# Attention by pairs of heads and one token tile, heads alternating between halves of the TensorE array

## The chip, the cores and the metric

The kernel runs on one core of one Trainium2 chip. The metric is the device time of one execution in microseconds, as the median of several executions; lower is better. TensorE (PE in the profile) multiplies, VectorE (DVE) and ScalarE (ACT) do the elementwise work and empty PSUM, GpSimd (POOL) does little here, and SyncE (SP) issues the DMAs.

## The reference

Two blocks follow each other on 256 tokens of width 1024. The first has a layer with a recurrence and a retention, and a layer with sparse attention (NSA); each has an FFN. The second has two layers with two attention branches of four heads each (`a` and `d`), a Fourier branch and a spatial gate; its first layer does the same for 256 context tokens, whose keys and values both layers attend to. Cut to what the change touches:

```python
# retention, a chunk of 128 tokens at a time, 8 heads of 64
s = jnp.einsum('bhid,bhjd->bhij', qf, kf) * inner_decay
o = jnp.einsum('bhij,bhjd->bhid', s, vf) + ...
# NSA: 16 heads of 64, 4 groups of keys; selected blocks, window, compressed keys
p_slc = jax.nn.softmax(s, axis=-1)...
o_slc = jnp.einsum('bgrqkl,bgqkld->bqgrd', p_slc, vg)
p_win = jax.nn.softmax(jnp.where(band, s, NEG), axis=-1)
o_win = jnp.einsum('bgrqk,bkgd->bqgrd', p_win, vw)
o = gb[..., 0:1] * o_cmp + gb[..., 1:2] * o_slc + gb[..., 2:3] * o_win
# second block, per branch; k and v are context and own tokens; sink in branch d
s = jnp.einsum('bqkgd,bnkd->bkgqn', q, k)
p = jax.nn.softmax(jnp.concatenate([s, s_sink], axis=-1), axis=-1)[..., :-1]
o = jnp.einsum('bkgqn,bnkd->bqkgd', p, v)
```

## The kernel before, in words

All weights are streamed from HBM in pieces of 512 KB, and each piece is split into two float32r parts, `whi` by ACT and `wlo` by DVE (lines 339 and 340). A product in these parts is three matmuls (`mm3`, lines 420 to 422: low times high, high times low, high times high). A product in plain float32 (`mm`, line 425) is one matmul in the code; the trace has two MATMUL rows for it. Most of the time goes to such products on the whole 128 by 128 array.

A head has 64 columns. Scores contract over 64 features, so their matmuls use half of the array's rows: the first half for the even head of a pair, the second for the odd one (`r0`). The product with the values has 64 output features, so it uses half of the array's columns. The trace writes a whole-array matmul `128*128`, one on half of the rows `64*128`, one on half of the columns `128*64`.

- **Retention** (`hybrid`, lines 759 to 773): a loop over 8 heads; scores into a bank of PSUM `P` (line 764), times the decay on DVE (766 and 767), times the values (769 to 771). Two heads go with each of four steps of the product for `g`.
- **NSA** (`nsa`, from 994): a unit is one head, the even or the odd one (`half`) of a pair `p`, and both token tiles: `scores(p, half)` makes them, 256 keys wide for the first and 512 wide for the second, in two `P` banks. `softmax(p, half, s)` takes the maximum with the mask (1012), the exponential (1015), and scales by the gates (1021), in the buffer `C3` (`Es`). Then come six transposes (1038) into two `Q` banks, copies to SBUF by ACT (1041) and DVE (1042), and the product with the values into `po`, the free half of a score bank. After the second unit of a pair, `split` writes `po` to `oT`. The scores of unit k + 2 and the softmax of unit k + 1 are issued around the work of unit k.
- **Attention of the second block** (`attend`, from 1136): the same with units `(p, half)` and both token tiles in a unit; `X` is the main stream, `C` the context's. In `X` the scores are 512 wide over two key tensors, 12 matmuls of 256 columns for each unit in two `R` banks; the values' products (`weigh`) are four of 256 columns. In `C` both token tiles of a head share one bank.

What runs beside it: generators yield after each piece of work, and `beside`, `bg` and `side_by` step the context's stream and the modulation beside the main path. The tile framework's scheduler then sets the order of each engine's instructions; each engine takes them in that order and waits on semaphores.

Of the kernel before, what the change touches and what calls it, by code (L numbers as in the profile page):

```python
# [13 lines left out]
OP = mybir.AluOpType  # L14
# [10 lines left out]
# ---------------------------------------------------------------- host side: layout and constants  # L25
# [197 lines left out]
def _bd(w):  # L223
    """[2n, 64, 64] -> [128, n * 128], pairs on a block diagonal."""
# [8 lines left out]
def _params(i):  # L233
    """Per-partition parameters and small operands, each [128, n]."""
# [29 lines left out]
def _rows(i):  # L264
    """Vectors along the free axis, to be spread over the partitions by DMA."""
# [30 lines left out]
# ---------------------------------------------------------------- device side  # L296

class Weights:
    """A stream of weights: DMA of each piece, and its split into two float32r parts."""
# [7 lines left out]
    def keep(self, name, tags):  # L307
        """The next pieces of this name go to buffers of their own."""
# [37 lines left out]
def kernel(ctx: ExitStack, tc: tile.TileContext, x_in, ctx_in, wmain, wctx, wada, params, rows, tabs, out,  # L346
# [14 lines left out]
    # -- buffers  # L361
# [10 lines left out]
    class Env:  # L372
        """What a stream of work uses for itself: weights, a ring of short rows, and banks of PSUM."""
# [13 lines left out]
    def group(keys, src, place, tag, pool_=None):  # L387
        """neighbouring tables in one DMA; a view of each"""
# [18 lines left out]
    # -- small helpers  # L407
# [6 lines left out]
    def after_marks():  # L414
        """what follows is issued after the last split"""
# [31 lines left out]
    def beside(g, *others):  # L447
        """the work g, with a step of the others after each of its own"""
# [12 lines left out]
    def behind(seen):  # L461
        """what follows is issued after the first split of a weight since"""
# [8 lines left out]
    def rms_factor(env, src, junk, after=None):  # L471
        """One token tile [128, 1024]: the factor of each row."""
# [53 lines left out]
    def f_out(env, o, xf, name):  # L526
        """128 output features on partitions: o [128, 256]."""
# [6 lines left out]
    def f_two(env, xf, name, acc=None):  # L534
        """256 output features, two blocks side by side in one bank."""
# [30 lines left out]
    class Out:  # L566
        """1024 output features along the free axis; the rows of the weight come one tile at a time."""
# [19 lines left out]
        def flush(self, gs):  # L587
            """the products held, for these groups: token tile g % 2 of operand g // 2"""
# [24 lines left out]
    def rope(dst, src, tc_, ts_, h, b, c, ta_, tb_):  # L613
        """dst = src * cos + swapped(src) * sin; rows of h heads, each b blocks of two halves of c."""
# [12 lines left out]
    # ------------------------------------------------------------ first block  # L627
# [26 lines left out]
    def recur_params(ga_b, gx_b, lam):  # L654
        # softplus(-lam) = max(-lam, 0) + log1p(exp(-|lam|)), log1p by the series of atanh
# [21 lines left out]
    def hybrid(hook):  # L677
# [23 lines left out]
        # recurrent branch  # L701
# [13 lines left out]
        def recur():  # L715
# [13 lines left out]
            # a = exp(-X), tp = tanh(X/2): 1 - a = tp (1 + a), which keeps its digits where X is small  # L729
# [15 lines left out]
        # retention branch  # L745
# [13 lines left out]
        def retention():  # L759
            for h in range(8):  # L760
                r0 = slice(64 * (h % 2), 64 * (h % 2) + 64)
                s = psum("P")
                mm(s[:, 0:256], kT[r0, h // 2, 0:128], qT[r0, h // 2, :])
                mm(s[:, 256:384], kT[r0, h // 2, 128:256], qT[r0, h // 2, 128:256])
                st = X.tmp(384)
                dve.tensor_mul(st[:, :256], s[:, :256], decay[:, h * 256:(h + 1) * 256])
                dve.tensor_mul(st[:, 256:], s[:, 256:384], decay[:, h * 256:h * 256 + 128])
                hc = slice(64 * h, 64 * h + 64)
                mm(ro[0][:, hc], st[:, 0:128], vv[:, 0, hc])
                mm(ro[1][:, hc], st[:, 128:256], vv[:, 0, hc], True, False)  # L770
                mm(ro[1][:, hc], st[:, 256:384], vv[:, 1, hc], False, True)
                yield

        ret = retention()
        o = yield from beside(t_out(X, xf, "g", 512), ret, ret, rec)
# [27 lines left out]
        gn = group_norm(rp)  # L803
# [19 lines left out]
    def nsa(hook, pre):  # L823
# [8 lines left out]
        def rope16(v, t, h):  # L832
            """in place on the first 16 of 64 columns of h heads; v [128, h * 64]"""
# [6 lines left out]
        # keys: columns of kT are slc1 slc0 win0 win1; the compressed ones of two groups on a block diagonal  # L840
# [14 lines left out]
        # compressed keys and values  # L855
# [67 lines left out]
        # queries  # L923
# [23 lines left out]
        def compressed():  # L947
            """the probabilities over the compressed keys, all heads at once, times the gates"""
# [45 lines left out]
        def scores(p, half):  # L994
            """of token tiles 0 and 1; the first leaves half a bank"""
            r0 = slice(64 * half, 64 * half + 64)
# [7 lines left out]
        def softmax(p, half, s):  # L1004
            """the probabilities of both token tiles times the gates"""
            E = Es[:, half]
            mx, rs = X.small(4, "mx"), X.small(4, "rs")
            parts = [(2 * t + i, s[t][:, i * w:i * w + w], E[:, c + i * w:c + i * w + w], m)
                     for t, w, c, ms in ((0, 128, 0, (nsa_m[:, 128:256],) * 2), (1, 256, S, (nsa_m[:, 128:384], nsa_m[:, 0:256])))
                     for i, m in enumerate(ms)]  # L1010
            for k, z, e, m in parts:
# [574 lines left out]
```

## Time and profile before

| | |
|---|---|
| executions, us | 1486.92, 1484.84, 1478.87 |
| median, us | 1484.84 |
| span of the profiled execution, us | 1487.6 |
| PE busy in the span | 1434.1 us, 96% |
| PEld (weight loads) busy | 1274.3 us, 86% |
| DVE busy | 969.4 us, 65% |
| ACT busy | 715.2 us, 48% |
| mean granted TensorE clock | 0.985 |

The span runs from the first to the last instruction of one execution; a time for what lies around it is not shown, and the median of the three executions lies 2.8 us below it. A PE row's duration is how long one matmul takes from start to end. Matmuls are pipelined, so what one costs in a row of them is the distance from its start to the next one's start.

### The profile page before, as it was taken

How to read it: one execution, taken by the hardware profiler on the slowest of the kernel's cores; microseconds unless marked ns; L12 is line 12 of the kernel's file. 1: busy time of each engine (PE TensorE's matmuls, PEld its weight loads, DVE VectorE, ACT ScalarE, POOL GpSimd, SP SyncE). 2: the span in 40 equal slices, each digit the busy share in tenths (PEclk: the TensorE clock that was granted, in tenths of full speed). 3: DMA queues.
4: the chain of work that ended last, by engine and by line, in shares of the span. 5: the costliest groups of instructions: out<-in, count | busy, mean ns of one | idle time of the engine just before them, and what ended most of it. 6: DMA issues, size and time to landing. Idle time of an engine off the chain costs nothing. (4 is left out here: it accounts for less than half of the span.)

```text
span 1487.6 us, 23997 instructions
## 1 busy us (share of the span) xinstructions
PE 1434.1 (96%) x9591; PEld 1274.3 (86%) x9591; DVE 969.4 (65%) x1747; ACT 715.2 (48%) x1206; POOL 39.2 (3%) x46
## 2 busy tenths in 40 slices
PE   7998999999999999999998999999999999999998
PEld 6777889988797668999887888899999878879997
DVE  7867887645676767768786765443443667764566
ACT  5643435556455654544445565333333346653443
POOL 0000000000100000000000100000000001100000
PEclk9999999999998999999999999999999999999999
DMA  8635776545453007676775442133333526413563
GB/s 288 205 120 188 249 239 231 171 139 175 131 149 108 1 30 225 216 240 229 233 254 177 150 128 86 59 120 107 113 103 126 156 62 185 146 55 101 184 186 126
DMA packets 65745, 230.30 MB, mean 155 GB/s; under 512 B 7776, under 2 KB 9312, under 8 KB 65376
## 3 DMA queue, kind: packets, MB, share of 16 engines
q1 hardware_dynamic: 65632, 228.76, 48.2%
q8 instruction: 75, 1.23, 0.3%
q14 instruction: 38, 0.31, 0.1%
HBM read 227.68 MB, written 1.05 MB: 154 GB/s over the span
## 5 line engine op out<-in xcount | busy, mean ns | idle before, releaser
L340 DVE TENSOR_TENSOR wlo<-raw,whi 128x1024 fp32r<-128x1024 f32 (+2 forms) x325 | 392.3, 1210 | 181.0 <-ACT whi L339 179.3
L339 ACT ACTIVATE whi<-raw 128x1024 fp32r<-128x1024 f32 (+2 forms) x325 | 340.2, 1048 | 323.3 <-PE P L422 80.5
L420 PE MATMUL P<-B,wlo 128*128 128x256 f32 x752 | 216.2, 288 | 0.0
L421 PE MATMUL P<-B,whi 128*128 128x256 f32 x752 | 214.2, 285 | 0.0
L422 PE MATMUL P<-B,whi 128*128 128x256 f32 x752 | 213.7, 284 | 0.0
L420 PE MATMUL Q<-B,wlo 128*128 128x256 f32 x704 | 203.3, 289 | 4.7 <-DVE wlo L340 4.1
L421 PE MATMUL Q<-B,whi 128*128 128x256 f32 x704 | 201.1, 286 | 0.0
L422 PE MATMUL Q<-B,whi 128*128 128x256 f32 x704 | 201.0, 286 | 0.0
L420 PEld LDWEIGHTS P<-B,wlo 128*128 128x128 f32 x752 | 144.0, 192 | 4.1 <-issue 3.0
L421 PEld LDWEIGHTS P<-B,whi 128*128 128x128 f32 x752 | 144.0, 191 | 3.7 <-issue 3.5
L422 PEld LDWEIGHTS P<-B,whi 128*128 128x128 f32 x752 | 143.9, 191 | 1.0 <-issue 0.8
L420 PEld LDWEIGHTS Q<-B,wlo 128*128 128x128 f32 x704 | 136.6, 194 | 9.2 <-DVE wlo L340 6.1
L421 PEld LDWEIGHTS Q<-B,whi 128*128 128x128 f32 x704 | 136.8, 194 | 1.7 <-issue 0.4
L422 PEld LDWEIGHTS Q<-B,whi 128*128 128x128 f32 x704 | 136.6, 194 | 0.3
L420 PE MATMUL P<-whi,B 128*128 128x512 f32 (+3 forms) x264 | 102.1, 388 | 5.1 <-DVE B L411 5.1
L421 PE MATMUL P<-wlo,B 128*128 128x512 f32 (+3 forms) x264 | 99.4, 378 | 0.4 <-DVE wlo L340 0.4
L422 PE MATMUL P<-whi,B 128*128 128x512 f32 (+3 forms) x264 | 99.2, 376 | 0.0
L1072 DVE SCALAR_TENSOR_TENSOR M<-raw,silu_c,M 128x1024 f32<-128x1024 f32 x42 | 53.9, 1282 | 41.3 <-DMA raw<-in_wada_dram 41.1
L420 PE MATMUL R<-C,wlo 128*128 128x256 f32 x272 | 76.2, 280 | 0.0
L421 PE MATMUL R<-C,whi 128*128 128x256 f32 x272 | 76.0, 279 | 0.0
L422 PE MATMUL R<-C,whi 128*128 128x256 f32 x272 | 75.9, 279 | 0.0
L420 PE MATMUL P<-whi,fp 128*128 128x512 f32 x160 | 62.3, 411 | 5.2 <-ACT whi L339 5.2
(494 smaller groups left out, 2958.9 us busy)
## 6 DMA issues: line engine op xcount, KB each, us to landing
raw<-in_wmain_dram SPq DMA_DIRECT2D x324, 512.0 KB, 4.0
raw<-in_wada_dram SPq DMA_DIRECT2D x48, 512.0 KB, 4.3
raw<-in_wctx_dram SPq DMA_DIRECT2D x26, 512.0 KB, 3.9
raw<-in_wmain_dram SPq DMA_DIRECT2D x8, 384.0 KB, 3.1
F<-in_rows_dram SPq DMA_DIRECT2D x4, 512.0 KB, 5.1
C<-in_ctx_dram SPq DMA_DIRECT2D x2, 1024.0 KB, 4.8
C<-in_params_dram SPq DMA_DIRECT2D x3, 512.0 KB, 4.3
ring<-in_rows_dram SPq DMA_DIRECT2D x6, 256.0 KB, 4.5
```

The source lines that it names most:

```text
L339: self.nc.scalar.activation(hi, src, AF.Copy)
L340: self.los.append(self.nc.vector.tensor_sub(lo, src, hi).ins)
L420: pe.matmul(o, l[1], r[0], start=first, stop=False)
L421: pe.matmul(o, l[0], r[1], start=False, stop=False)
L422: pe.matmul(o, l[0], r[0], start=False, stop=last)
L1072: dve.scalar_tensor_tensor(a, t, mods[nm][:, k:k + 1], a, OP.mult, OP.add)
```

## The change

A unit is now a pair of heads and one token tile. The two heads' matmuls are issued alternately: scores on the first and the second half of the rows, into two banks (`halves3`, `mm` in retention), values on the first and second half of the columns, into two halves of one bank. Each value product is 128 columns wide for one token tile where it was 256 for two, so there are twice as many of them. In NSA `po` has a `P` bank of its own, and the copies out of `Q` go to DVE for the first token tile and to ACT for the second. In the second block the small DVE operations of two heads are merged. In retention the scores move to `R` banks, and the scores of the next pair are issued before the step that waits for the decay. Comments were removed too.

```diff
+    def halves3(os, ls, rs):
+        for k, (a, b) in enumerate(((1, 0), (0, 1), (0, 0))):
+            for o, l, r in zip(os, ls, rs):
+                pe.matmul(o, l[a], r[b], start=k == 0, stop=k == 2)
+    HALF = slice(0, 64), slice(64, 128)
...
         def retention():
-            for h in range(8):
-                r0 = slice(64 * (h % 2), 64 * (h % 2) + 64)
-                s = psum("P")
-                mm(s[:, 0:256], kT[r0, h // 2, 0:128], qT[r0, h // 2, :])
-                mm(s[:, 256:384], kT[r0, h // 2, 128:256], qT[r0, h // 2, 128:256])
+            def scores(i):
+                ss = psum("R"), psum("R")
+                for c, kc, qc in ((slice(0, 256), rows128(0), A), (slice(256, 384), rows128(1), rows128(1))):
+                    for r0, s in zip(HALF, ss):
+                        mm(s[:, c], kT[r0, i, kc], qT[r0, i, qc])
+                return ss
...
+                yield
+                for st, hc in sts:
+                    mm(ro[0][:, hc], st[:, 0:128], vv[:, 0, hc])
...
+                if i < 3:
+                    ss = scores(i + 1)
...
-        o = yield from beside(t_out(X, xf, "g", 512), ret, ret, rec)
+        o = yield from beside(t_out(X, xf, "g", 512), ret, rec)
...
-            mm3(s[0][:, :S], sub(qT, r0, p, rows128(0)), sub(kT, r0, p // 4, slice(128, 384)), True, True)
-            mm3(s[1], sub(qT, r0, p, rows128(1)), sub(kT, r0, p // 4), True, True)
+            c, w = ((slice(128, 384), S), (A, 512))[t]
+            halves3([z[:, :w] for z in s], [sub(qT, r0, p, rows128(t)) for r0 in HALF],
+                    [sub(kT, r0, p // 4, c) for r0 in HALF])
...
-        Es = buf("C3", [2, 768])
+        Es = buf("C3", [3, 512])
+        Es = halves(Es[:, 0]), Es[:, 1:3]
...
-                po = ss[p, 1][0][:, S:]
+                po = psum("P")[:, :S]
...
-            for br in range(2):
-                c0 = br * 256 + gcol
-                mm(po[r0], vv[:, 0, c0:c0 + 64], pa_s[:, br * 256:br * 256 + 256], False, False)
-                mm(po[r0, 128:], vv[:, 1, c0:c0 + 64], pb_s[:, br * 128:br * 128 + 128], False, br == 1)
+            for j, (br, kt) in enumerate(blocks):
+                for h, r0 in enumerate(HALF):
+                    c0 = br * 256 + (2 * gp + h) * 64
+                    mm(po[r0, rows128(t)], vv[:, kt, c0:c0 + 64], at(pTs, h, j), False, t == 1 and j == nb - 1)
...
-        def probs(p, half):
+        def probs(p, t):
+            s = psum(env.sc), psum(env.sc)
+            for i, kp in enumerate(kT):
+                halves3([z[:, i * S:(i + 1) * S] for z in s], [sub(qT, r0, p, rows128(t)) for r0 in HALF],
+                        [sub(kp, r0) for r0 in HALF])
...
-            for j in range(nj):
-                mm(o[r0, :S], vs[j][:, r0], pT[j // 2][:, (j % 2) * S:(j % 2 + 1) * S], j == 0, j == nj - 1)
+            for j in range(nj):
+                for h, r0 in enumerate(HALF):
+                    mm(o[r0, rows128(t)], vs[j][:, r0], at(pTs, h, j), j == 0, j == nj - 1)
```

On PE in the attention of layer 0 of the second block, before: the values' products of one unit (`vc` the context's values, `T` the own ones) stand between whole-array products.

```order
L420 MATMUL P<-B_7993,wlo 128x256
L425 MATMUL P<-ring,vc_2393 64x256 x2
L421 MATMUL P<-B_7994,whi 128x256
...
L421 MATMUL P<-B_7994,whi 128x256
L425 MATMUL P<-ring,T_8120 64x256 x2
L422 MATMUL P<-B_7993,whi 128x256
```

The same place in the change, with the scores of a later unit (`kc` context keys, `cq` own keys) around it:

```order
L428 MATMUL R<-kc_2392,C_8114 128x256 x3
L428 MATMUL R<-cq,C_8114 128x256 x3
L428 MATMUL R<-kc_2392,C_8114 128x256 x3
L428 MATMUL R<-cq,C_8114 128x256
L431 MATMUL P<-ring,vc_2393 64x128 x4
L431 MATMUL P<-ring,T_8116 64x128 x4
L428 MATMUL R<-cq,C_8114 128x256 x2
L420 MATMUL P<-B_7989,wlo 128x256
L1207 MATMUL Q<-ident,ring 128x128 x8
```

The eight value products of a unit stand together, the two heads alternating; the scheduler has put one head's six score matmuls ahead of the other's, and has parted the last two of them from their partners.

On PE in NSA, with buffer numbers (`F0`, `vc1`: the compressed branch, which opens `po`), in the change, at the first two pairs:

```order
L431 MATMUL P_4539<-F0_4338,vc1_3912 128x256
L428 MATMUL P_4564<-M1_3720,M3_3916 128x256
L428 MATMUL P_4564<-M1_3720,M2_3915 128x256 x2
...
L428 MATMUL P_4565<-M1_3720,M3_3916 128x256
L428 MATMUL P_4565<-M1_3720,M2_3915 128x256 x2
L428 MATMUL P_4622<-M1_3720,M3_3916 128x512
L428 MATMUL P_4622<-M1_3720,M2_3915 128x512 x2
L1055 MATMUL Q_4541<-ident_79,C3_4494 128x128 x4
L428 MATMUL P_4623<-M1_3720,M3_3916 128x512
L428 MATMUL P_4623<-M1_3720,M2_3915 128x512 x2
L431 MATMUL P_4539<-ring_4546,fp_4339 64x128 x4
```

`P_4564` and `P_4565` are the two heads of one unit, `P_4622` and `P_4623` those of the unit after it: other work stands between the halves of each, and both units' scores stand ahead of the first value product of the pair before (`P_4539`).

On PE in retention, before, the scores of two heads, then at once what needs their decay:

```order
L425 MATMUL P<-M_413 128x256
L425 MATMUL P<-M_413 128x128
L425 MATMUL P<-M_413 128x256
L425 MATMUL P<-M_413 128x128
L420 MATMUL P<-whi,B_88 128x512
L425 MATMUL Q<-M_551,ring 128x64 x3
```

and in the change, where these rows follow twelve whole-array matmuls on the scores before them:

```order
L422 MATMUL P<-whi,B_87 128x512
L431 MATMUL Q<-M_551,ring 128x64 x6
L431 MATMUL R<-M_413 128x256 x2
L431 MATMUL R<-M_413 128x128 x2
L420 MATMUL P<-whi,B_88 128x512
```

## Rows read from the trace of the kernel before

**Rows 1.** The page, part 1, and TensorE's granted clock in 40 slices.

```profile
PE 1434.1 (96%) x9591; PEld 1274.3 (86%) x9591; DVE 969.4 (65%) x1747; ACT 715.2 (48%) x1206; POOL 39.2 (3%) x46
...
PEclk9999999999998999999999999999999999999999
```

**Rows 2.** NSA, layers 0, 1: length, busy PE, PEld, DVE, ACT, POOL; clock, DMA, GB/s.

```profile
462.00:551.00 89.00, 85.74 (x475) 58.02 (x473) 63.18 (x293) 57.63 (x194) 0.00 (x0) 0.98 0.08 26
860.00:980.00 120.00, 117.54 (x821) 101.97 (x821) 61.41 (x136) 58.75 (x100) 1.33 (x1) 0.97 0.27 84
1285.00:1362.00 77.00, 74.48 (x492) 60.81 (x490) 45.83 (x118) 39.80 (x72) 0.00 (x0) 1.00 0.25 76
```

**Rows 3.** Timeline of PE in layer 0's attention: start, us, then instruction.

```profile
911.82 1.08 PE L425 MATMUL P<-ring,vc 128*64 128x256 f32 x4
912.83 0.39 PE L422 MATMUL P<-B,whi 128*128 128x256 f32 x1
```

**Rows 4.** Timeline of PE in NSA, values of one unit (four 256 wide, four 128).

```profile
503.36 1.51 PE L425 MATMUL P<-ring,fp 128*64 128x256 f32 x8
504.81 0.50 PE L422 MATMUL P<-M,M 64*128 64x512 f32 x1
```

**Rows 5.** Timeline of PE in layer 0's spatial gate, where column halves alternate already.

```profile
979.84 1.09 PE L425 MATMUL Q<-M,fp 128*64 128x128 f32 x16
980.87 0.38 PE L420 MATMUL P<-B,wlo 128*128 128x256 f32 x1
```

**Rows 6.** Timeline of PE at the start of NSA, scores of both heads of a pair.

```profile
465.18 0.51 PE L420 MATMUL P<-M,M 64*128 64x256 f32 x2
465.41 0.28 PE L421 MATMUL P<-M,M 64*128 64x256 f32 x1
465.52 0.28 PE L422 MATMUL P<-M,M 64*128 64x256 f32 x1
465.53 0.39 PE L421 MATMUL P<-M,M 64*128 64x512 f32 x1
```

**Rows 7.** Timeline of PE, scores of one head in layer 0.

```profile
901.68 0.28 PE L420 MATMUL R<-cq,C 64*128 64x256 f32 x1
901.80 0.28 PE L421 MATMUL R<-cq,C 64*128 64x256 f32 x1
```

**Rows 8.** Line 425 by tile: duration min/median/max in ns, first and last start, forms.

```profile
L425 PE MATMUL P<-ring,fp x128: 272/379/686, 473.5 to 552.7; 128*64 128x256 f32 x64, 128*64 128x128 f32 x64
...
L425 PE MATMUL P<-ring,vc x64: 379/379/686, 884.2 to 1346.2; 128*64 128x256 f32 x64
```

**Rows 9.** Retention, who waited for line 766: us in total, times.

```profile
  PE Q L425: 3.2, 4
```

**Rows 10.** Timeline of PE in retention: whole array, both heads' scores, whole array.

```profile
67.82 0.39 PE L421 MATMUL P<-wlo,B 128*128 128x512 f32 x1
68.05 0.39 PE L422 MATMUL P<-whi,B 128*128 128x512 f32 x1
68.37 0.93 PE L425 MATMUL P<-M 64*128 64x256 f32 x8
69.23 0.50 PE L420 MATMUL P<-whi,B 128*128 128x512 f32 x1
```

**Rows 11.** NSA, DVE and ACT groups by form: xcount, busy us, mean ns, idle before.

```profile
L1012 DVE CUSTOM_DVE_ANT_0 C<-P,T 128x256 f32<-128x256 f32 x32 | 12.7, 418 | 5.0 <-PE P L422 5.0
L1021 DVE TENSOR_TENSOR C<-C,rs 128x512 f32<-128x512 f32 x16 | 10.9, 684 | 0.0
...
L1015 ACT ACTIVATE C<-C,mx 128x256 f32<-128x256 f32 x32 | 15.8, 495 | 0.0
L1041 ACT ACTIVATE ring<-Q 128x512 f32<-128x512 f32 x16 | 9.4, 590 | 7.0 <-PE Q L1038 6.9
```

**Rows 12.** Busy time by stretch at the start of NSA, columns as in the second group.

```profile
470.00:473.00 3.00, 1.93 (x12) 1.27 (x11) 2.58 (x13) 2.85 (x13) 0.00 (x0) 1.00 0.34 124
473.00:476.40 3.40, 3.40 (x11) 1.82 (x10) 2.39 (x9) 1.90 (x10) 0.00 (x0) 0.51 0.00 0
```

More of the change, by code (lines that the diff above doesn't have):

```diff
@@ L1023, in nsa @@
-        units = [(p, half) for p in range(8) for half in range(2)]
+            dve.tensor_tensor(rs, rs, gates[:, t, 4 * p:4 * p + 4], OP.mult)
+            dve.tensor_tensor(e4, e4, rs.unsqueeze(2).to_broadcast([128, 4, w]), OP.mult)
+        units = [(p, t) for p in range(8) for t in range(2)]
         ss = {u: scores(*u) for u in units[:2]}
         softmax(*units[0], ss[units[0]])
-        for k, (p, half) in enumerate(units):
+        for k, (p, t) in enumerate(units):
             gp = p // 4
-            r0 = slice(64 * half, 64 * half + 64)
@@ new lines, in nsa @@
+            nb = len(blocks)
+            pts = [psum("Q") for _ in range(t + 1)]
+            at = lambda zs, h, j: zs[(h * nb + j) // 4][:, rows128((h * nb + j) % 4)]
+            for h in range(2):
+                for j in range(nb):
+                    pe.transpose(at(pts, h, j), Es[t][:, h, rows128(j)], ident)
+            yield
+            pTs = [X.tmp(512) for _ in pts]
+            if t == 0:
+                dve.tensor_copy(pTs[0], pts[0])
+            else:
+                for z, pt in zip(pTs, pts):
+                    act.activation(z, pt, AF.Copy)
@@ L1144, in probs @@
             Es = []
-            for t in range(2):
-                s = s2[:, t * S:(t + 1) * S] if one_bank else psum(env.sc)
-                for i, kp in enumerate(kT):
-                    mm3(s[:, i * S:(i + 1) * S], sub(qT, r0, p, rows128(t)), sub(kp, r0), True, True)
+            mx, rs = env.small(2, "mx"), env.small(2, "rs")
+            sk = None if sink is None else sink[:, 2 * p:2 * p + 2]
+            for h in range(2):
+                c = slice(h, h + 1)
                 E = env.tmp(513)
@@ L1167, in probs @@
-                dve.reciprocal(rs, rs)
-                dve.tensor_scalar(E[:, :nk], E[:, :nk], rs, None, OP.mult)
-            return Es
-        def weigh(o, half, pT):
-            r0 = slice(64 * half, 64 * half + 64)
-            for j in range(nj):
-                mm(o[r0, :S], vs[j][:, r0], pT[j // 2][:, (j % 2) * S:(j % 2 + 1) * S], j == 0, j == nj - 1)
-        units = [(p, half) for p in range(2) for half in range(2)]
+                    dve.tensor_tensor_reduce(E[:, :nk], s[h][:, :nk], mask[t], 1.0, sk[:, c], OP.add, OP.max, mx[:, c])
@@ L1177, in attend @@
+            dve.reciprocal(rs, rs)
+            for h, E in enumerate(Es):
+                dve.tensor_scalar(E[:, :nk], E[:, :nk], rs[:, h:h + 1], None, OP.mult)
+            return Es
+        at = lambda zs, h, j: zs[(h * nj + j) // 4][:, rows128((h * nj + j) % 4)]
+        units = [(p, t) for p in range(2) for t in range(2)]
         Es = {units[0]: probs(*units[0])}
         yield
-        pTs = {}
-        for k, (p, half) in enumerate(units):
-            if not one_bank and k < 3:
+        for k, (p, t) in enumerate(units):
+            if not one and k < 3:
@@ L1182, in attend @@
                 Es[units[k + 1]] = probs(*units[k + 1])
-            if not one_bank and half == 0:
+            if not one and t == 0:
                 o = psum(env.out)
             pts = [psum(env.tr) for _ in range(nj // 2)]
-            for t in range(2):
+            for h in range(2):
                 for j in range(nj):
-                    c0 = (j % 2) * S + t * 128
-                    pe.transpose(pts[j // 2][:, c0:c0 + 128], Es[p, half][t][:, rows128(j)], ident)
-            pTs[half] = [env.tmp(512) for _ in pts]
@@ L1191, in attend @@
-            for i, pT in enumerate(pTs[half]):
+                    pe.transpose(at(pts, h, j), Es[p, t][h][:, rows128(j)], ident)
+            pTs = [env.tmp(512) for _ in pts]
+            for i, pT in enumerate(pTs):
                 if i == 0:
@@ L1195, in attend @@
                     dve.tensor_copy(pT, pts[i])
-            if not one_bank:
-                weigh(o, half, pTs[half])
             yield
-            if half == 1:
-                if one_bank:
-                    o = psum(env.out)
-                    for h in range(2):
-                        weigh(o, h, pTs[h])
-                    dve.tensor_mul(yb[:, base + p], o[:, :S], z[:, p])
-                else:
-                    yf = env.tmp(S)
-                    dve.tensor_mul(yf, o[:, :S], z[:, p])
-                    split(yf, *sub(yb, A, base + p))
-                yield
-            if one_bank and k < 3:
-                Es[units[k + 1]] = probs(*units[k + 1])
+            if one:
+                o = psum(env.out)
+            for j in range(nj):
+                for h, r0 in enumerate(HALF):
+                    mm(o[r0, rows128(t)], vs[j][:, r0], at(pTs, h, j), j == 0, j == nj - 1)
+            if one:
+                dve.tensor_mul(yb[:, base + p, rows128(t)], o[:, rows128(t)], z[:, p, rows128(t)])
+                if t == 1:
+                    yield
+                if k < 3:
+                    Es[units[k + 1]] = probs(*units[k + 1])
+                    yield
+            elif t == 1:
+                yf = env.tmp(S)
+                dve.tensor_mul(yf, o[:, :S], z[:, p])
+                split(yf, *sub(yb, A, base + p))
                 yield
```

88 lines of the change are left out of this document (38 added, 50 removed).

## The prediction

> **What bounds the kernel now.** I read the page first. PE is busy 96% of the span and no other engine is above 65% [rows 1], and the granted clock is at its upper level, 2.4 GHz, in nearly every slice. That average hides stages, so I read the stretches in which attention runs next [rows 2]. In layer 0 and layer 1 PE is busy 117.5 of 120 us and 74.5 of 77, while DVE and ACT have about half of the time left: there the time is PE's. In NSA PE is busy 85.7 of 89 us, but DVE has 63.2 and ACT 57.6, so PE leads there by less. A busy PE is not yet a full PE, so the third view is its timeline, where the distance between starts says what a matmul costs.
>
> Four value products of 256 columns hold PE from 911.82 to 912.83, 1.01 us [rows 3]. Four of 256 and four of 128 hold it 1.45 us [rows 4]. The difference, 0.44 us, is four of 128, 0.11 each, so one of 256 costs 0.22 and 0.13 is left, which I take as the price of going into and out of the half-array form. In the spatial gate sixteen of 128 hold PE 1.03 us [rows 5]: less that 0.13, 0.90 us for sixteen, or 0.11 for **two**. That code already alternates the two halves of the columns, in the same type and width that the change gives to the value products: two run in the time of one.
>
> For the halves of the rows, the start of NSA is the nearest row: a 256-wide matmul of one head starts at 465.52 and a 512-wide one of the other at 465.53, and the 256-wide ones keep their pace beside the 512-wide ones, 0.11 us from 465.41 to 465.52 [rows 6]. One head alone takes 0.12 for such a step [rows 7]. So row halves run side by side too, and their weight loads with them.
>
> **The change part by part.** What limits the gain is the scheduler: partners overlap only where no whole-array matmul stands between them. I counted in the order of the change, stretch by stretch between whole-array matmuls, how much of each kind lies beside work of the other half.
>
> - *Values, second block, X.* Before: 128 rows of 256 (64 with `vc` [rows 8], 64 with `T`), 128 x 0.22 = 28.2 us, none overlapped. After: 256 of 128, the same columns; 88% lie beside a partner, which saves half of that share: 28.2 x 0.44 = 12.4 us.
> - *Values, NSA.* 64 x 0.22 + 64 x 0.11 [rows 8] = 21.1 us before; 85% overlapped after: 9.0 us.
> - *Values, context.* 32 x 0.22 = 7.0 us; 25% overlapped before, 94% after: 2.4 us.
> - *Scores, X.* 192 x 0.12 = 23.0 us [rows 7]; none before, 60% after: 6.9 us.
> - *Scores, NSA and context.* NSA has 48 of 256 and 48 of 512 (0.23 us each, as whole-array ones [rows 10]), 48 x 0.12 + 48 x 0.23 = 16.8 us; the order of before already overlaps 34% (as at 465.5), that of the change 52%: 1.5 us. Context: 48 x 0.12 = 5.8 us, 17% after: 0.5 us.
> - *Going in and out of half arrays.* 222 changes of form in the order before, 219 after: nothing at 0.13 each.
> - *Retention.* PE waits 3.2 us for the decay [rows 9]. In the new order twelve whole-array matmuls stand between the scores and what needs them, 2.8 us at 0.23 each, so the decay is done when it is asked for. I take 3.0 us. Its scores overlap already: eight matmuls, 4 x 0.22 + 4 x 0.11 = 1.3 us if alone, take 0.86 [rows 10]. Moving them to other banks costs nothing while `R` is free there.
> - *DVE, ACT.* DVE has 72 fewer instructions, ACT three fewer table loads; both lie beside PE, so nothing in X; in NSA this is a small help.
> - *DMA, SP.* SP's order is the same in both. Nothing.
>
> The PE terms come to 32.7 us, with retention 35.7.
>
> *What comes late next.* In NSA about 12 us of PE work goes (9.0 + 1.5 and half of the context's 2.9), and the stage would be 77 us long, with 63 us of DVE work and 58 us of ACT work in it that hardly shrinks. The longest serial piece of a pair is now the second tile's softmax: four maxima, four exponentials and a product of twice 512, 4 x 0.42 + 4 x 0.50 + 2 x 0.68 = 5.0 us [rows 11], then eight transposes (0.9) and two copies on one engine (2 x 0.59), where there was one. That is about 7.1 us and as much as 9 with the small operations, against 77 / 8 = 9.6 us for a pair. So some of the gain comes back as waits. Bounds: nothing, as PE hardly waits for softmax now, and 12 us, all of it. Where PE does wait, 470 to 473, the clock behind it stands at 1.2 GHz until 476.4 [rows 12], 3.4 us that cost 1.7; two or three more such places are inside these bounds. I take 5, nearer to nothing, since both units' scores stand ahead of the value product before them.
>
> Sum: 35.7 - 5 = 30.7, rounded to 30 us. The profiled span is 1487.6, which gives 1457.6; the median of the three executions lies 2.8 below that span, and I take the saving from the median: 1484.84 - 30 = **1455 us**.
>
> The Trainium skill speaks for less: "TensorE: Matmul & The Clock Gate", section "Measured speedup vs the span model", gives 3.07 times for four row tiles and 2.38 for three column tiles, under four fifths of the ideal; an estimate from it for two halves is 1.6 times, which would leave three quarters of the 32.7, and a time near 1462. This trace does not agree for column halves, 0.11 us for two and 0.11 for one [rows 4, 5].
>
> **The rivals.**
>
> *NSA is bound by DVE and ACT* (20%). All that PE saves there turns into waits: 30.7 + 5 - 12 leaves 23.7, less two clock drops of 1.7 the gain is about 20: 1465 us. For it: 63 of 89 us on DVE. Against it: before the change DVE and ACT wait for PE there, 5.0 us at line 1012 and 7.0 at 1041 [rows 11]. The same skill's "TensorEngine Tiling (Array Packing)", section "PSUM Bottleneck", says that tiling speeds up TensorE but not the emptying of PSUM; by that rule it comes out so.
>
> *Row halves do not overlap, column halves do* (6%). Then the scores' 8.9 us are lost, and the wait in NSA is shorter: 35.7 - 8.9 - 3 = 23.8, 1461 us. Against it: rows 6, though they are one place.
>
> *Nothing overlaps* (6%). The change would then only cut the same columns into twice as many matmuls; retention's 3 us are left: 1482 us, no measurable change. Against it: rows 5 and 6.
>
> *NSA's units follow one another* (5%), the one that is slower. `po` takes a `P` bank of its own, so a pair asks for five banks of four, where it asked for four. If scores then wait for the bank of a `po` that is not yet split, DVE and ACT take turns instead of working at once: 63.2 + 57.6 = 121 us [rows 2] against 89, 32 more. X's 19.3 and retention's 3 are kept, the context's 2.9 lost: 1484.84 + 32 - 22 = 1495 us. It decides once NSA grows by more than 22 us, that is, with two thirds of the overlap gone. Against it: in the order, the scores of two units stand ahead of the value product of the pair before.
>
> **How the numbers follow.** My forecast has the remaining 63%. What a measurement can tell from no change is 0.5%, 7.4 us. Faster by more than that: 63 + 20 + 6 = 89%; the same: 6%; slower: 5%. The range begins where nothing comes back in NSA and a few more partners overlap than the order promises (41 us, 1444) and reaches past the two cases at 1461 and 1465 with the spread of the executions of before, 6 us below the median and 2 above it, to 1472. It leaves out no overlap and the slower case, 11%, and some of the ends.
>
> **What would show it.** The 128-wide value products in pairs, sixteen in about 1.0 us; layers 0 and 1 shorter by about 10 us each with PE still at 97% busy; no wait of PE for the decay; NSA at 80 to 84 us with PE's busy share lower and DVE's higher. I am wrong if the pairs start 0.11 us apart one after another, if PE's waits for DVE or ACT in NSA exceed 12 us, or if the clock's slices there show more than a few at 1.2 GHz.

## The result, and the profile after

| | before | after |
|---|---|---|
| median, us (4 executions each) | 1482.05 | 1459.33 |
| lowest and highest | 1478.87 to 1486.92 | 1457.47 to 1460.63 |
| span of the profiled execution | 1487.6 | 1456.3 |

The change is faster by 1.6%: ratio 0.9841, 95% interval 0.982 to 0.9862, that is 20 to 27 us less. The forecast was 1455 (1444 to 1472).

The page of after, part 1 and the granted clock [rows 1]:

```profile
PE 1402.7 (96%) x9815; PEld 1265.0 (87%) x9815; DVE 962.7 (66%) x1675; ACT 710.2 (49%) x1203; POOL 38.6 (3%) x46
...
PEclk9999999999998999999999999999999999999999
```

PE is as full as it was; 31 us of it are gone. The windows of after between the same whole-array matmuls as in [rows 2], NSA, layer 0, layer 1, and then a piece of layer 1:

```profile
454.10:534.00 79.90, 75.06 (x533) 54.50 (x531) 59.36 (x257) 56.08 (x191) 0.00 (x0) 0.96 0.12 34
845.70:952.20 106.50, 105.54 (x899) 98.12 (x899) 59.56 (x121) 57.85 (x99) 1.32 (x1) 1.00 0.33 96
1256.10:1332.00 75.90, 71.95 (x573) 62.84 (x572) 44.97 (x103) 40.15 (x75) 0.00 (x0) 0.93 0.26 77
1267.00:1277.30 10.30, 8.63 (x46) 7.45 (x47) 5.59 (x12) 5.83 (x11) 0.00 (x0) 0.51 0.17 52
```

NSA lost 9.1 us and layer 0 lost 13.5, but layer 1 only 1.1, and its clock is 0.93 where it was 1.00. The last row shows why: 10.3 us at a granted clock of 0.51, that is at 1.2 GHz.

The timeline of PE in layer 0 of after, the values of one unit [rows 3]:

```profile
913.90 0.66 PE L431 MATMUL P<-ring,vc 128*64 128x128 f32 x8
914.38 0.61 PE L431 MATMUL P<-ring,T 128*64 128x128 f32 x8
914.92 0.61 PE L428 MATMUL R<-kc,C 64*128 64x256 f32 x3
```

Sixteen rows of 128 columns hold PE for 1.02 us, as in the spatial gate [rows 5]: the column halves run two at a time. In NSA eight take 0.59 and fourteen 1.01 [rows 4]:

```profile
474.61 0.66 PE L431 MATMUL P<-ring,fp 128*64 128x128 f32 x8
475.20 0.49 PE L428 MATMUL P<-M,M 64*128 64x512 f32 x1
...
480.12 1.09 PE L431 MATMUL P<-ring,fp 128*64 128x128 f32 x14
481.13 0.66 PE L1055 MATMUL Q<-ident,C 128*128 128x128 f32 x4
```

Scores in X, both heads of a unit together in layer 1, then one head that the scheduler has parted from the other, in layer 0 [rows 7]:

```profile
1281.33 0.62 PE L428 MATMUL R<-cq,C 64*128 64x256 f32 x6
1281.79 0.51 PE L428 MATMUL R<-M,C 64*128 64x256 f32 x6
1282.23 0.44 PE L1207 MATMUL Q<-ident,ring 128*128 128x128 f32 x2
```

```profile
896.05 0.62 PE L428 MATMUL R<-kc,C 64*128 64x256 f32 x3
896.51 0.51 PE L428 MATMUL R<-cq,C 64*128 64x256 f32 x3
896.95 0.38 PE L420 MATMUL P<-B,wlo 128*128 128x256 f32 x1
```

Twelve take 0.90 us and six take 0.90: a partner costs nothing, and a head alone pays the whole price and a change of form.

For the experiments, this table gives the distance between the same whole-array matmuls, in us, and in brackets how many of those us the clock was at 1.2 GHz. Such a stretch is counted as costing half its length, which is the most it can cost: where PE idles in it, as for 1.7 of the 10.3 us above, it costs less. The stretches are wider than the windows above, so their differences are not the same.

```
                       retention  to NSA       NSA          to layer 0   layer 0    layer 1
before                 71.6(4.8)  268.9( 8.9)  154.7(13.7)  293.3(10.2)  97.3(6.8)  76.4( 0.0)
after                  69.0(2.4)  264.5( 7.9)  148.6(17.1)  292.9( 6.8)  82.6(0.0)  73.9(10.2)
nsa_of_before          69.1(2.3)  266.4(11.3)  153.4(10.2)  295.8(10.2)  82.7(0.0)  72.7( 6.8)
attend_of_before       69.4(4.4)  266.1( 2.4)  147.2(10.2)  290.1(10.2)  96.9(6.8)  76.4( 0.0)
retention_of_before    74.3(8.4)  266.1( 8.6)  143.9( 6.8)  290.4( 6.8)  82.6(0.0)  73.7(10.2)
pairs_bound            69.9(4.8)  269.2( 8.9)  139.0(13.7)  292.7( 6.8)  83.8(0.0)  71.2( 6.8)
pairs_bound_steps      69.2(3.9)  264.9( 6.3)  137.3(10.2)  292.4( 6.8)  83.7(0.0)  57.7( 0.0)
```

The context's attention lies in "to NSA" and beside NSA. In the last run layer 1's whole-array work is ordered otherwise, so its 57.7 is no like measure; between matmuls that keep their place around layer 1 the stretch is 108.9(10.2) in after, 106.2(6.8) in pairs_bound, 101.0(0.0) in steps_only and 100.9(0.0) in pairs_bound_steps.

### The profile page after: what moved, and what is told of

Read it like the earlier page. It is cut to its first block, busy times and chain, and to the rows that moved or that the text cites. A ratio compares the mean times of both kernels' runs of the same rounds, so it can differ in the third digit from the quotient of the medians.

```text
span 1456.3 us, 24385 instructions
## 1 busy us (share of the span) xinstructions
PE 1402.7 (96%) x9815; PEld 1265.0 (87%) x9815; DVE 962.7 (66%) x1675; ACT 710.2 (49%) x1203; POOL 38.6 (3%) x46
## 4 chain that ended last, share of the span: by engine, by line
PE 76%; DVE 9%; DMA 6%; ACT 5%; issue 3%; POOL 1%; SPq 0%; ACTq 0%; DVEq 0%; POOLq 0%
PE P L420 12%; PE P L421 12%; PE P L422 12%; PE Q L420 6%; PE Q L422 6%; PE Q L421 6%; PE R L420 4%; PE R L421 4%; PE R L422 4%; DVE wlo L340 3%; DMA raw<-in_wmain_dram 3%; PE P L431 3%; DMA raw<-in_wada_dram 2%; PE R L428 2%; PE Q L431 2%
```

## The experiments

"Less than before" is meant against executions of before beside the same run: median 1483.35 us for nsa_of_before, attend_of_before, pairs_kept and by_head, 1481.73 for retention_of_before, pairs_bound, steps_only and pairs_bound_steps, 1483.33 for the other four. The 95% interval of such a difference is 3 to 6 us to either side.

### Which part is worth what

*nsa_of_before*: the NSA units of before put back into the change, with their softmax and loop.

```diff
-        def scores(p, t):
+        def scores(p, half):
...
-        units = [(p, t) for p in range(8) for t in range(2)]
+        units = [(p, half) for p in range(8) for half in range(2)]
```

> The change with the NSA units of before; retention and the second block as in the change. My theory: NSA is worth what its stretch of the trace lost, 5 to 7 us (7.5 us of columns, less 2.5 us of changes of form and waits): 1465 us (1463 to 1468) against 1459. Rival: the gain in NSA went wholly into waits for DVE and ACT: 1459. Other rival: all 10.5 us that the order promises arrived: 1470.

1464.43 us (1463.38 to 1467.31) beside 1483.35 for before, 18.9 less, where the change has 22.7 less. In the executions NSA is worth some 4 us, in the trace 4.8; with half of the time at 1.2 GHz taken off, 148.3 against 140.1, 8 us. So the forecast was in the middle, and that the gain went wholly into waits is out by the stretch; by the executions alone, whose intervals just touch (0.986 to 0.9902, and 0.982 to 0.9862), it would not be.

*attend_of_before*: the function `attend` of before put back.

```diff
-        def probs(p, t):
+        def probs(p, half):
...
```

> The change with the attention of the second block (X and context) of before; retention and NSA as in the change. My theory: the columns of the two layers are worth 8 us each in the full-clock count of the trace and the context 2 to 3; the 14.6 us that layer 0 lost and the 2.4 that layer 1 lost differ by waits and half-clock stretches that fall by chance and cancel: 1459 + 18.5 = 1477 us (1473 to 1482). Rival: layer 0's whole 14.6 and layer 1's 2.4 belong to the change, with layer 1 bound by the scores' banks: the same sum of 17 to 20, but then the timeline of layer 0 here shows a stretch at half clock as in before, and that of layer 1 none.

1473.45 us (1469.41 to 1478.28), 9.9 less than before. The sum, 13 us, is smaller than either theory gave, but the stretches tell them apart: layer 0 is at 96.9 us again with 6.8 at 1.2 GHz, layer 1 at 76.4 with none, as in before. nsa_of_before and retention_of_before, with the new `attend`, have no such stretch in layer 0 and one in layer 1. So in these layers the stretches at 1.2 GHz are not chance, as I held, but belong to the order, as the rival had it. In before it begins so, by the waits of PE and a window of layer 0:

```profile
PE R L420 <- ACT ring L1163: 2.0, 2, 1.7
```

```profile
882.60:889.50 6.90, 6.90 (x25) 4.74 (x24) 3.92 (x9) 5.36 (x9) 0.00 (x0) 0.51 0.01 2
```

and in layer 1 of after, in its timeline (in brackets PE's idle time ahead, and who ended it) and its waits:

```profile
1263.21 0.28 PE L422 MATMUL P<-B,whi 128*128 128x256 f32 x1
1265.01 0.62 PE L428 MATMUL R<-cq,C 64*128 64x256 f32 x3 [1.52 <-ACT ring L1186]
...
1270.62 0.58 PE L428 MATMUL R<-cq,C 64*128 64x256 f32 x1 [1.52 <-ACT ring L1186]
```

```profile
PE R L428 <- ACT ring L1186: 3.0, 2, 1.5
PE Q L1207 <- DVE ring L1192: 0.5, 1, 0.5
```

The scores of the next unit wait for the exponentials that free the `R` banks, and PE has nothing else in its order; behind that it runs at 1.2 GHz until 1277.

*retention_of_before*: the loop over single heads put back.

```diff
-            for i in range(4):
+            for h in range(8):
...
-        o = yield from beside(t_out(X, xf, "g", 512), ret, rec)
+        o = yield from beside(t_out(X, xf, "g", 512), ret, ret, rec)
...
```

> The change with the retention loop of before (scores and what needs their decay next to each other, one head after the other). Theory: the wait for the decay comes back, 2.4 to 3 us: 1462 us (1460.5 to 1464), with PE waiting about 3 us for line 766's products in that stretch, and the rest of the stretch times as in the change. Rival: the wait was covered: 1459, no change.

1458.39 us (1456.18 to 1460.55) beside 1481.73: 23.3 less, as the change: the total is the rival's, and the forecast of 1462 missed. The wait is back in full, in the waits of PE in this stretch, first of after, then of this run [rows 9]:

```profile
PE R L815 <- DVE ring L812: 2.1, 2, 1.3
PE Q L431 <- DVE ring L780: 0.4, 1, 0.4
```

```profile
PE Q L431 <- DVE ring L773: 3.2, 4, 1.7
```

The stretch is 5.3 us longer, 2.3 without the clock. The total does not show it, since NSA has 6.8 us at 1.2 GHz here and 17.1 in after, a difference of 5 us that two profiled executions cannot put down to retention. So 2 us is read from the stretch, and the executions neither bear it out nor deny it.

### Only neighbours overlap: keeping pairs together

*pairs_kept*: each group of scores or values inside a critical section.

```diff
-        for k, (a, b) in enumerate(((1, 0), (0, 1), (0, 0))):
-            for o, l, r in zip(os, ls, rs):
-                pe.matmul(o, l[a], r[b], start=k == 0, stop=k == 2)
+        with tc.tile_critical():
+            for k, (a, b) in enumerate(((1, 0), (0, 1), (0, 0))):
+                for o, l, r in zip(os, ls, rs):
+                    pe.matmul(o, l[a], r[b], start=k == 0, stop=k == 2)
...
```

> The change with one thing more: the score matmuls of a pair of heads, and the value matmuls of a unit, are each bound into one group that the scheduler may not part. My theory: partners overlap exactly where no whole-array matmul stands between them, so the share that overlaps in the change (60% of the scores in X, 52% in NSA, about 85% of the values) goes to 100%. Counted in the new order that is 13 us of half-array columns less than in the change, and 177 changes of form where the change has 219, 42 x 0.13 to 0.2 = 5 to 8 us. 18 to 21 us less work on PE; up to 8 us of it come back as waits, since a score now waits for two banks at once: 1441 us (1437 to 1450) against 1459 for the change. Rival 1: attention is by now bound by DVE and ACT, the saving turns into waits of PE: 1453 to 1460, with PE's busy share lower. Rival 2: partners overlap also across whole-array matmuls, so nothing is to be had: 1457 to 1461, PE busy as in the change.

1672.6 us (1666.14 to 1677.5), ratio 1.1286: far off all theories, for a reason that none held: groups wait for things that they don't use. In the timeline values wait for the DMA of a weight, and the waits of PE have such rows on top:

```profile
1020.43 0.41 PE L420 MATMUL P<-B,wlo 128*128 128x256 f32 x1
1022.26 1.12 PE L432 MATMUL P<-ring,vc 128*64 128x128 f32 x8 [1.41 <-DMA raw<-in_wmain_dram]
```

```profile
PE R L429 <- DMA raw<-in_wmain_dram: 18.0, 5, 6.5
```

The 96 sections cost 2.2 us each in the end, (1672.6 - 1459.3) / 96, more than half of it through the clock: the mean granted clock is 0.91 where after has 0.985. On pairs the time of this run says nothing.

*pairs_bound*: the same without sections. The group's first matmul depends on the last reader of the banks (or on the copies) that the group needs.

```diff
+    def together(calls, *past):
+        calls = list(calls)
+        head = calls[0]()
+        for i in past:
+            tc.add_manual_dep(head.ins, i.ins.name, mybir.DependencyInfo(mybir.DependencyClass.Sync, mybir.DependencyReason.DATA),
+                              reason="together")
+        with tc.issue_after(head.ins), tc.high_priority(500):
+            for c in calls[1:]:
+                c()
...
```

> The change with pairs held together in another way than in pairs_kept, without critical sections: the first matmul of a group waits for what frees the last bank or copy that the group needs, and the rest of the group follows it at a raised priority. In the new order all NSA scores, all values and 75 to 87% of X's scores lie beside a partner: 10.2 us of half-array columns less than in the change, and 164 changes of form for 219, 55 x 0.13 to 0.2 = 7 to 11 us. My theory (only neighbours overlap, and PE still leads): 17 to 21 us less, some of which comes back as waits for two banks: 1443 us (1438 to 1452) against 1459. Rival 1: DVE and ACT bind by now, waits of PE take it all: 1455 to 1460 with a lower busy share of PE. Rival 2: holding a pair back delays the first head's softmax, and the waits outweigh the columns: above 1461.

1447.17 us (1443.45 to 1451.95), ratio 0.9754 (0.9729 to 0.9779): 34.6 less than before, 12 less than the change, as forecast. It comes in NSA, 139.0 us against 148.6 (132.2 against 140.1 without the clock); layer 0 has 83.8 against 82.6. NSA's window, to be read against the 79.9 us above:

```profile
459.90:533.70 73.80, 65.01 (x549) 48.54 (x548) 60.59 (x260) 55.27 (x194) 0.00 (x0) 0.98 0.11 37
```

PE is now busy 65 of 74 us there and DVE 61: only with all pairs together does the bound of the first rival come near.

*steps_only*: layer 1's attention advances evenly.

```diff
-        n1, n2, n3 = ((1, 1, 1), (1, 0, 2))[l]
+        n1, n2, n3 = ((1, 1, 1), (1, 1, 1))[l]
```

> The change with one line more: in layer 1 of the second block the attention advances by one step with each of the six groups of whole-array work, where it stood still for two of them and then took two at a time. In the order 18 to 33 whole-array matmuls then stand between a unit's scores and what waits for its softmax, at the start of layer 1 too. Theory: in the change layer 1 is 8 us shorter in columns, but PE waits 3.5 us there for the softmax of the first units, and the clock behind that is at 1.2 GHz for 10 us, which costs 5; without the wait both come back, and 2 us of overlap: 1459 - 10 = 1449 us (1446 to 1455), no half-clock stretch in layer 1. Rival: the clock there falls for another reason, or the wait only moves on: 1456 to 1460.

1450.37 us (1446.35 to 1452.14), ratio 0.978 (0.9756 to 0.9804): 31.4 less than before, 8.7 less than the change. Its window of layer 1 and its waits of PE there:

```profile
1256.00:1332.00 76.00, 74.62 (x659) 68.18 (x658) 48.66 (x102) 44.80 (x79) 0.00 (x0) 1.00 0.29 92
```

```profile
PE R L428 <- DVE mx L1174: 0.8, 1, 0.8
PE R L428 <- ACT ring L1186: 0.3, 1, 0.3
```

The waits went from 3.8 to 1.1 us and the clock is full. Around layer 1 the stretch went from 108.9 to 101.0 us, 7.9 of the 8.7. So the waits, and the clock that was low behind them, are the cause of layer 1's small gain. A wait of 1.5 us alone need not lower the clock: before has one in layer 1 (the row below), where its clock is 1.00 [rows 2].

```profile
PE R L420 <- ACT ring L1163: 1.6, 1, 1.6
```

*pairs_bound_steps*: both edits.

> pairs_bound and steps_only together. If the two gains are independent: 1459 - 16 - 9 = 1434 us (1429 to 1444). Rival: both removed the same waits in layer 1, then no better than the better one of the two, about 1443.

1441.89 us (1437.83 to 1446.16), ratio 0.9727 (0.9698 to 0.9756): 39.8 less than before, where the two gains alone would make 43.3: independent within the noise. *nsa_bound_steps* frees X's scores again (`plain` issues its calls one after another and binds nothing):

```diff
-            together(calls, *read[-2:])
+            plain(calls)
...
```

> pairs_bound_steps with X's scores set free again (the scheduler may part them, as in the change); NSA's scores and all values stay bound, layer 1's steps as in steps_only. By the stretches of the traces the binding is worth 8 us in NSA and nothing in the two layers (layer 0 83.7 against 82.6 us, layer 1 57.7 against 57.8): X's scores pay in waits for the second bank what they save in columns. So 1442 us, within 3 either way (1438 to 1445). Rival: X's binding was worth its 2 us of columns and 8 changes of form: 1445 to 1447. Other rival: the waits weigh more than the columns: 1437 to 1439.

1443.4 us (1440.93 to 1444.29), ratio 0.9726 (0.9706 to 0.9745), 39.9 less: the same. Binding X's scores is worth nothing. These two beat both kernels of this case.

*chained_steps*: in pairs_bound_steps, every matmul of a group is issued after the one ahead of it.

```diff
+            last = head
             for c in calls[1:]:
-                c()
+                with tc.issue_after(last.ins):
+                    last = c()
```

> pairs_bound_steps, but each group is one chain in alternating order, so that no matmul of one head can go ahead alone: 98% of X's scores on their own keys lie beside a partner where it was 87%, 1.7 us of columns less in the count. Theory: as in layer 0 before, what is saved comes back as waits for banks: 1441 us (1437 to 1445). Rival: columns are what counts: 1439.

1450.74 us (1445.46 to 1455.17), 32.6 less than before: a miss, 7 us slower than without the chain by these differences and 9 by the medians, with intervals that just touch. The profiled execution is its longest. By its waits of PE in layer 0, then those of pairs_bound_steps:

```profile
PE R L428 <- DVE mx L1196: 4.1, 2, 2.6
PE R L428 <- ACT ring L1208: 2.1, 2, 1.9
PE R L420 <- DVE mx L1196: 1.9, 1, 1.9
```

```profile
PE R L428 <- ACT ring L1204: 2.1, 2, 1.9
PE R L428 <- DVE mx L1192: 1.7, 1, 1.7
```

More columns overlap, more is waited for banks, and layer 0 has 10.2 us at 1.2 GHz there: 86.5 us against 83.7. Of a pair held back too strictly the wait, with the low clock, costs more than the columns. Without the chain layer 0 waits too (the second block of rows), and its clock stays up: 83.7(0.0) in the table.

### Is it alternating that counts, or being neighbours?

*by_head*: pairs_kept with one head's matmuls ahead of the other's.

```diff
-            for k, (a, b) in enumerate(((1, 0), (0, 1), (0, 0))):
-                for o, l, r in zip(os, ls, rs):
+            for o, l, r in zip(os, ls, rs):
+                for k, (a, b) in enumerate(((1, 0), (0, 1), (0, 0))):
...
```

> As pairs_kept, but inside a group one head's matmuls come first and then the other's, instead of alternating. Theory A: each half of the array works off its own line of matmuls, and being neighbours is what counts: same time as pairs_kept within 0.5%, the second head's first matmul starting beside the first head's first. Theory B: PE starts matmuls in program order, so that only alternating ones overlap: then only the one at the seam of the two heads overlaps, 22 us of scores and 24 us of values are lost, about 1485 us. Mixed outcomes would be rows as in A and columns as in B: about 1463, or the reverse: about 1461; the timeline tells these apart (eight 128-wide value products in 0.45 us of starts or in 0.9; six 256-wide scores in 0.36 or in 0.72).

1679.44 us (1676.8 to 1683.9), under the same sections, so only the groups are compared, from their first start to the start of what follows, at full clock: three scores of a head and three of the other take 0.72 us for 0.70 in pairs_kept, but eight and eight value rows take 1.66 for 1.18. Neither A nor B. Hence two runs on pairs_bound, *heads_in_turn* (all of one head, then all of the other) and *by_twos* (two products of one head, then two of the other, where 2 stands for the 8 below), both chained as in chained_steps:

```diff
+        a, b = calls[0::2], calls[1::2]
+        calls = [c for k in range(0, len(a), 8) for c in a[k:k + 8] + b[k:k + 8]]
...
```

> pairs_bound, but inside each group the first head's matmuls come first and then all of the second's. In by_head, eight value rows of one head followed by eight of the other ran so that the second head's first row started beside the first head's fifth; four and four ran as fast as alternating ones. Theory: PE lets a matmul of the other half start past at most four waiting ones. Then nothing is lost where a head has four rows (NSA's first tile, the context), four steps of 0.11 us in the 24 groups with eight value rows per head, 24 x 0.43 = 10.3 us, and two steps of 0.12 in the 16 score groups of X with six rows per head, 3.8 us: 1447 + 14 = 1461 us (1456 to 1465). If the halves ran fully on their own: 1447. If only matmuls next to each other in program order overlap: 24 us of values and 20 of scores lost, 1491.

1459.03 us (1457.6 to 1463.32), ratio 0.9843 (0.9818 to 0.9868): 12 slower than pairs_bound by the medians, 10 by the differences from before, near the 14 forecast. The total also holds the chain and other waits (in layer 0 they sum to 2.5 us, for 5.8 in pairs_bound), so overlap is read from the groups. In this order the chain leaves pairs and changes of form as they were, 164. Its timeline shows the values of one unit (the first head's `vc` x4 and `T` x4, then the second's) and its scores (`kc` x3, `cq` x3 of each head):

```profile
911.23 0.65 PE L451 MATMUL P<-ring,vc 128*64 128x128 f32 x4
911.72 0.27 PE L451 MATMUL P<-ring,T 128*64 128x128 f32 x1
911.73 0.32 PE L451 MATMUL P<-ring,vc 128*64 128x128 f32 x1
...
912.21 0.60 PE L451 MATMUL P<-ring,T 128*64 128x128 f32 x4
912.74 0.38 PE L428 MATMUL R<-kc,C 64*128 64x256 f32 x1
```

```profile
853.37 0.73 PE L428 MATMUL R<-kc,C 64*128 64x256 f32 x4
853.83 0.28 PE L428 MATMUL R<-cq,C 64*128 64x256 f32 x1
...
854.61 0.39 PE L420 MATMUL P<-whi,B 128*128 128x256 f32 x1
```

The second head's first value row, 911.73, starts with the first head's fifth, 911.72: three of the first head are still waiting, and it goes past them (the expectation counted four). The fourth `kc` row of the scores is the second head's first; it starts at 853.715, 6 ns behind the first head's third, again past three. The values take 1.51 us for 1.02, the scores 1.24 for 0.90.

> pairs_bound, but the two heads alternate by two products at a time (two rows of scores, four rows of values), each group chained in this order, which also keeps a few more of X's scores beside a partner (1.7 us of columns less, three changes of form less). Theory (a reach of four): two by two overlap as well as one by one: 1447 - 2 = 1445 us (1441 to 1449). If only neighbours in program order overlap, half of the overlap of values and scores is lost, some 20 us: 1467.

1456.53 us (1452.99 to 1457.1): the total is off by 11 us, between the two theories. The group is not, by its timeline:

```profile
867.48 0.67 PE L451 MATMUL P<-ring,vc 128*64 128x128 f32 x8
867.97 0.66 PE L451 MATMUL P<-ring,T 128*64 128x128 f32 x8
868.56 0.33 PE L1229 MATMUL Q<-ident,ring 128*128 128x128 f32 x1
```

1.08 us for sixteen, so two by two overlap nearly as alternating ones do. What is slower is the chain: its waits in layer 0 are those of chained_steps (4.1, 2.0 and 1.9 us), and layer 0 takes 86.9 us with 10.2 at 1.2 GHz. The theory of a reach stands, with three for four; the price of the chain I had not seen.

## Why the prediction was right, point by point

*The sum.* 30.7 us were forecast and the profiled spans differ by 31.3. By stretches, at full clock (half of the brackets taken off): retention 1.4, the context's part 3.9, NSA 7.8, layer 0 11.3, layer 1 7.6, together 32.0; the stretch ahead of layer 0 gives 1.3 back. The us at 1.2 GHz in these stretches sum to 44.4 in both traces, so in these two executions the clock moved and did not change the sum. But the medians differ by 22.7 only (20 to 27), so the match of the spans is in part luck: the profiled execution of before, with a span of 1487.6 us, is longer than the longest of its four times, 1486.92, where in the runs below a span is some 2 us shorter than its time. The record has the span and the mean granted clock of every execution, and their product is an estimate of its length at full clock. By it 25 executions of before, those beside the experiments, take 1465 us and lose another 16 to the clock; the four of after take 1436 and lose 21. So 28.5 us went at full clock, and 5 of them came back as time at 1.2 GHz. The term that was too small is what comes back: I took 5 us in all, for NSA alone. That 1459 still lies near 1455 is luck too: I started from a median that was 2.8 us high, as a fourth execution showed (1482.05 for 1484.84), and that hides 2.8 of the 7 us by which the saving fell short.

*Values and scores in X*, 12.4 + 6.9 = 19.3: 11.3 + 7.6 = 18.9 measured. Right, with full overlap of neighbours and nothing for the others; the waits of PE in the two layers' windows sum to 4.7 us in both traces, so this is work.

*Layers 0 and 1 about 10 us each, PE 97% busy*: wrong in both: 14.7 and 2.5 by the table, PE 99% and 95% busy. The step that failed is the count of PE's work alone, with the waits of before taken as staying where they are. The new order took a wait of 1.7 us and 6.8 us at 1.2 GHz out of layer 0; in layer 1 it raised the waits from 2.5 to 3.8 us and brought 10.2 us at 1.2 GHz; steps_only shows the second.

*NSA at 80 to 84 us*: 79.9. Of some 12 us of PE work 7.8 came, so 4 were given back where I took 5. PE's busy share fell from 96 to 94% of the stretch, as said. Its waits there are now 4.4 us, all for DVE, where before they summed to 2.6, so they account for 1.8 of the 4; the rest was not traced. (L1179 and L1189 are the context's attention, which runs beside.)

```profile
PE P L428 <- DVE mx L1029: 1.3, 3, 0.7
PE Q L1055 <- DVE rs L1189: 1.1, 1, 1.1
PE Q L1055 <- DVE mx L1179: 1.0, 1, 1.0
PE Q L1055 <- DVE C L1036: 0.6, 1, 0.6
PE P L431 <- DVE ring L1059: 0.4, 1, 0.4
```

The rival that DVE and ACT bind did not come; pairs_bound got 8 us more out of the same stage. In the executions the old NSA units (nsa_of_before) take 1446 us at full clock by the estimate above, for after's 1436, and lose 4 us less to the clock: that is why the medians show less than the stretch.

*Context*, 2.9, half of it ahead of NSA: 3.9 there. With the old `attend` the same stretch takes 264.9 us at full clock, before 264.5 and after 260.6, so all of it is the attention's, more than its columns; what the rest is was not tried.

*Retention*, 3.0: the wait went from 3.2 to 0.4 us as forecast, but the transposes behind it wait 0.8 us longer, and the stretch gained 1.4 to 2.3.

*Changes of form* at nothing: the traces have the 222 and 219 that I counted. Eight value rows take 0.59 us and sixteen 1.02, so eight more cost 0.44 and 0.15 is left for going in and out, where I had 0.13. Scores with 0.90 for twelve at 0.117 a pair leave 0.20.

*The rivals.* Neither "nothing overlaps" nor "row halves do not": twelve scores take the time of six. Nor did the clock in NSA fall far: 0.96 for 0.98. The slower one had units follow one another; NSA is shorter, not longer. The estimate of 1.6 times from the Trainium skill's "TensorE: Matmul & The Clock Gate", section "Measured speedup vs the span model", does not hold for two halves here: 0.70 for six pairs of score rows, 0.70 for six alone, once the changes of form are off. The median lies nearer to that estimate's 1462 than to 1455, so the total does not decide this; the rows do.

*Open.* Where the clock falls in NSA differs from run to run by up to 10 us of 1.2 GHz, and no run here says which of its small waits decides it. Nor is it known which wait does it in the layers: 1.6 us in before's layer 1 and 1.9 in pairs_bound_steps' layer 0 were followed by no low clock, 1.7 in before's layer 0 was. By the estimate above the old NSA units, the old `attend` or layer 1's even steps each bring the loss to the clock back to some 16 us, as in before, so the three do not add.

## What to carry to other kernels

Work on two halves of the array runs in the time of one, rows as well as columns, but only inside a stretch without whole-array matmuls: count the pairs in the scheduled order, not in the code, and bind those that the scheduler parts (it was worth 8 us in NSA and nothing for X's scores), with a dependency on what the second one waits for, not with a critical section and not as a chain. Then look for the waits that the new order makes: in layer 1 waits of 3.8 us, with 10.2 us at 1.2 GHz behind them, cost 8 us, though waits as long elsewhere were followed by no low clock, so read the clock of each stretch. Judge a stage by its own stretch with the clock taken off, since the clock's stretches move by more than a term of 3 us.

## What the runs showed of the hardware that I had not expected

PE starts a matmul for the free half past three waiting ones of the other half, in rows and in columns (911.73 and 853.715 above), so heads need not alternate one by one: two products by two (four rows by four) take 1.08 us for sixteen value rows, four and four, as a whole group, 0.594 for 0.587, three and three scores 0.72 for 0.70, and eight and eight lose half of the overlap (1.51 for 1.02). The Trainium skill's "TensorE: Matmul & The Clock Gate", section "The mechanism", has matmuls start and end in program order; the timelines of heads_in_turn differ from that between the two halves, and by that rule, as an estimate, its sixteen value rows would take some 1.8 us (15 steps of 0.11 and 0.15), not 1.51. The measurement decides.

Retention's eight score rows of two heads, not alternating in before, alternating in after, take 0.86 and 0.85 us [rows 10].
